# One power for both token tiles of a query/key group, and its mean squares first in line, in a four-layer trunk

## The chip, the core and the metric

The kernel runs on one core of a Trainium2 chip. TensorE (PE) does matrix products and transposes, VectorE (DVE), ScalarE (ACT) and GpSimd (POOL) the rest, SyncE (SP) issues the weight loads. Each engine works through its own queue in order and waits on semaphores for the others. The metric is the device time of one execution, in microseconds (us); smaller is better.

## The reference

Four pre-norm residual layers over an input of 256 tokens by 1024 features, in float32. Layers 0 and 3 are a gated MLP with a causal mix inside chunks of 128 tokens, layer 2 is causal pooling, and layer 1 is the attention layer that the change touches:

```python
def mixer_b(h, w_in, q_gain, k_gain, w_out):
    proj = h @ w_in
    qkv = proj[..., :n_qkv].reshape(bsz, S, 3, N_B_GROUPS, B_HEADS, HEAD_DIM)
    z = proj[..., n_qkv:]
    for g, (window, dilation) in enumerate(B_PATTERNS):        # 3 groups
        q = apply_partial_rotary(rms_norm(qkv[:, :, 0, g], q_gain[g]), cos, sin)
        k = apply_partial_rotary(rms_norm(qkv[:, :, 1, g], k_gain[g]), cos, sin)
        o, lse = dilated_window_attention(q, k, qkv[:, :, 2, g], window // dilation, dilation)
        ...
    # groups combined by softmax over lse, times silu(z), then @ w_out
```

`rms_norm` divides each head's 128 values of a token by the root of their mean square plus 1e-6 and multiplies by a gain. There are 8 heads and 3 groups, so 24 query heads and 24 key heads are normalised for each of the 256 tokens.

## The kernel before

**Products.** Every matrix product is made of three matmuls of fp32r halves (`mm3`, lines 77 to 79): each operand is split into a high part (written by ACT with a copy, `hi_of`, line 82) and a low part (what is left, written by DVE, `lo_of`, line 85). The weights come as 272 units of 512 KB: loaded by SP into four raw buffers (`wr`), split into `w<n>h` and `w<n>l` in seven buffers, and used by PE in order. The splitting runs five units ahead of the use (`AHEAD`).

**Order.** One Python program writes the instructions of all engines. PE's main stream is a row of projections; `step` is called after every six matmuls of 512 columns (or twelve of 256) and calls `tick`. Everything else is a task, a generator that hands out its next piece when its due tick has come: `tick` goes through the list of tasks in the order in which they were spawned, so an older task's piece stands ahead of a younger one's on each engine. After `tick`, `step` splits the next weight unit.

**The attention layer.** Heads go in four pairs (`hp` 0 to 3). For each pair PE projects queries and keys of the two heads for group 0, 1 and 2 (one `qk` projection each, both token tiles t=0 and t=1 of 128 tokens at once), then the values. Each `qk` projection spawns a `qk_task(hp, g, o)`, twelve in all; tiles are named by pair and group, so `qk10` is pair 1, group 0. A `qk_task` goes as follows, with the ticks between its pieces:

- `square(0)`, `square(1)`: ACT squares 128 columns of each of four heads and sums them (line 508; four `ACTIVATE` with four accumulator reads for each tile), into `qs`.
- two ticks later `rms(0)`, `rms(1)`: DVE makes mean squares `qm` from `qs` (line 512), POOL raises them to the power -0.5 into `qr` (line 513, a `tensor_tensor` with a constant tile). Each of both is done once for each token tile, on 128x4 values.
- one tick later `scale(0)`, then `scale(1)` with `rotate(0)`, then `rotate(1)`: ACT multiplies the four heads by `qr` into `qn` (line 517), DVE applies the rotary part (lines 526 to 531).
- two ticks later `transpose(0)`: PE transposes `qn` (line 538) into a PSUM tile `qt`, ACT writes the high part `qk..h` with the gain (line 540); a tick later `low(0)`: DVE writes the low part (line 546); a tick later `transpose(1)`, a tick later `low(1)`.

The PSUM tile `qt` comes from a tag with one buffer (`trp`). So PE's `transpose(1)` has to wait until DVE's `low(0)` of the same task has read the tile, and both stand two ticks apart.

Because one `qk` projection has eight ticks and a `qk_task` needs more than that, `low(1)` of one task and `rms` of the next fall due in the same tick, wherever two `qk` projections or a `qk` projection and a value projection follow each other. In the list the older task, with its `low(1)`, comes first.

Of the kernel before, what the change touches and what calls it, by code (L numbers as in the profile page):

```python
# [14 lines left out]
ALU = mybir.AluOpType  # L15
# [8 lines left out]
EPS = 1e-6  # L24
HD = 128
# [23 lines left out]
def hybrid_trunk_kernel(ctx, tc, x, wts, norm_gainT, a_v_gain, a_wsT, a_bsT, b_gl, b_gv, c_scaleT,  # L49
                        masks, rope, rcnt, out):  # L50
    nc = tc.nc
# [10 lines left out]
    def trp(name):  # L62
        return ps.tile([P, HALF], F32, tag="tr", name=name, bufs=1)
# [4 lines left out]
    def tiny(n, name, tag="t"):  # L68
        return cp.tile([P, n], F32, tag=f"{tag}{n}", name=name, bufs=8)

    def pair(pool, shape, tag, name, bufs):
        return (pool.tile(shape, F32R, tag=tag + "h", name=name + "h", bufs=bufs),
                pool.tile(shape, F32R, tag=tag + "l", name=name + "l", bufs=bufs))
# [15 lines left out]

    tasks = []  # L90
    now = [0]

    def spawn(gen, delay=0):
        if delay == 0:
            try:
                delay = next(gen)
            except StopIteration:
                return
        tasks.append([now[0] + delay, gen])

    def tick():
        now[0] += 1
        for e in list(tasks):
            if e[0] <= now[0]:
                try:
                    e[0] = now[0] + next(e[1])
                except StopIteration:
                    tasks.remove(e)
# [3 lines left out]
    def need(key):  # L112

        n = 0
        while key not in done:
            tick()
            n += 1
            assert n < 1000, (key, sorted(map(str, done)), [(e[1].__name__, e[1].gi_frame.f_lineno) for e in tasks])
# [44 lines left out]
    def step(i, ahead=AHEAD):  # L163

        tick()
        if i % 2 == 0:
            split_hi(used[0] + ahead)
        else:
            split_units(used[0] + ahead)
# [14 lines left out]
    m05_row = cp.tile([P, 32], F32, tag="m05", name="m05")  # L184
    nc.gpsimd.memset(m05_row, -0.5)
    m05 = m05_row[:, :4]
# [72 lines left out]
    def proj_tok(name, skew=None):  # L259

        o = [pp(f"{name}_{t}") for t in range(2)]
        if skew is not None:
            ws = [next_unit() for j in range(4)]
            for t in range(2):
                need(("h", skew, t))
                for k in range(KT):
                    w = ws[k // 2]
                    mm3(o[t], h_t(k, t), (w[0][:, k % 2], w[1][:, k % 2]), k == 0, k == KT - 1)
                    if k % 2:
                        tick()  # L270
                        if t == 1:
                            split_units(used[0] + min(k // 2 + 1, W_BUFS - 4))
            return o
        for j in range(4):
            w = next_unit()
            for kk in range(2):
                k = 2 * j + kk
                for t in range(2):
                    mm3(o[t], h_t(k, t), (w[0][:, kk], w[1][:, kk]), k == 0, k == KT - 1)
                step(kk)  # L280
        return o
# [74 lines left out]
    def layer_a(layer, consts, pl, mid):  # L356
# [3 lines left out]
        def tmp(tag, name, bufs):  # L360
            return pl.tile([P, HALF], F32, tag=tag, name=name, bufs=bufs)

        vs = [tiny(4, f"vs{layer}{t}") for t in range(2)]
        v = []
        wsr = []

# [123 lines left out]
    def layer_b(layer, consts, pl):  # L490
# [7 lines left out]
        def qk_task(hp, g, o):  # L498
            qh, ql = pair(pl, [P, 4, S], "qk", f"qk{hp}{g}", 4)
            qk[hp, g] = (qh, ql)  # L500
            ssq = [tiny(4, f"qs{hp}{g}{t}") for t in range(2)]
            rq = [tiny(4, f"qr{hp}{g}{t}") for t in range(2)]
            qn = [pl.tile([P, 4, HD], F32, tag="qn", name=f"qn{hp}{g}{t}", bufs=2) for t in range(2)]
            ov = [o[t].rearrange("p (h d) -> p h d", d=HD) for t in range(2)]

            def square(t):
                for h in range(4):
                    nc.scalar.activation(junk[:, :HD], ov[t][:, h], AF.Square, accum_out=ssq[t][:, h:h + 1])  # L508

            def rms(t):  # L510
                ms = tiny(4, f"qm{hp}{g}{t}")
                nc.vector.tensor_scalar(ms, ssq[t], 1.0 / HD, EPS, op0=ALU.mult, op1=ALU.add)  # L512
                nc.gpsimd.tensor_tensor(rq[t], ms, m05, op=ALU.pow)  # L513

            def scale(t):
                for h in range(4):
                    nc.scalar.activation(qn[t][:, h], ov[t][:, h], AF.Copy, scale=rq[t][:, h:h + 1])  # L517

            def rotate(t):

                ra = pl.tile([P, 4, ROPE], F32, tag="ra", name=f"ra{hp}{g}{t}", bufs=1)
                rb = pl.tile([P, 4, ROPE], F32, tag="rb", name=f"rb{hp}{g}{t}", bufs=1)
                for a in range(2):
                    hs = slice(2 * a, 2 * a + 2)
                    c = rop[:, 0, t, g, a:a + 1, :].to_broadcast([P, 2, ROPE])
                    nc.vector.tensor_tensor(ra[:, hs], qn[t][:, hs, :ROPE], c, op=ALU.mult)  # L526
                    for b in range(2):
                        s0, s1 = b * 16, (1 - b) * 16
                        c = rop[:, 1, t, g, a:a + 1, s0:s0 + 16].to_broadcast([P, 2, 16])
                        nc.vector.tensor_tensor(rb[:, hs, s0:s0 + 16], qn[t][:, hs, s1:s1 + 16], c, op=ALU.mult)  # L530
                nc.vector.tensor_tensor(qn[t][:, :, :ROPE], ra, rb, op=ALU.add)

            pts = [None, None]

            def transpose(t):
                pts[t] = trp(f"qt{hp}{g}{t}").rearrange("p (h c) -> p h c", c=P)
                for h in range(4):
                    nc.tensor.transpose(pts[t][:, h], qn[t][:, h], ident)  # L538
                for a in range(2):
                    nc.scalar.activation(qh[:, 2 * a:2 * a + 2, t * P:(t + 1) * P], pts[t][:, 2 * a:2 * a + 2],  # L540
                                         AF.Copy, scale=gv[:, 2 * g + a:2 * g + a + 1])

            def low(t):
                for a in range(2):
                    d = (slice(None), slice(2 * a, 2 * a + 2), slice(t * P, (t + 1) * P))
                    nc.vector.scalar_tensor_tensor(ql[d], pts[t][:, 2 * a:2 * a + 2], gv[:, 2 * g + a:2 * g + a + 1],  # L546
                                                   qh[d].bitcast(F32), op0=ALU.mult, op1=ALU.subtract)

            square(0)
            square(1)  # L550
            yield 2
            rms(0)
            rms(1)
            yield 1
            scale(0)
            yield 1
            scale(1)
            rotate(0)
            yield 1
            rotate(1)  # L560
            yield 2
            transpose(0)
            yield 1
            low(0)
            yield 1
            transpose(1)
            yield 1
            low(1)
            if g == NG - 1:
                spawn(score_task(hp, 0), 1)  # L570
                spawn(score_task(hp, 1), 3)
# [135 lines left out]
        for hp in range(NHEAD // 2):  # L707
            for g in range(NG):
                spawn(qk_task(hp, g, proj_tok(f"qk{hp}{g}", skew=layer if hp == 0 and g == 0 else None)))
                if hp == 0 and g == 0:  # L710
                    gate(0)
                    gate(1)
            o = proj_tok(f"v01{hp}")
            vh, vl = pair(pl, [P, 2, HALF], "v01", f"v01{hp}", 1)
            spawn(val_task(hp, o, vh, vl))
            vp = pp(f"v2p{hp}")
            for j in range(2):
                w = [a.rearrange("p a b -> p (a b)") for a in next_unit()]
                for kk in range(4):
                    k = 4 * j + kk  # L720
                    ws = [a[:, kk * 256:(kk + 1) * 256] for a in w]
                    for t in range(2):
                        mm3(vp[:, t * 256:(t + 1) * 256], h_t(k, t), ws, k == 0 and t == 0, k == KT - 1)
                    if kk % 2:
                        step(kk // 2)
            v2h, v2l = pair(pl, [P, 2, 256], "v2", f"v2{hp}", 1)
            spawn(val2_task(hp, vp, v2h, v2l))
            spawn(mix_task(hp, (vh, vl, v2h, v2l), szT[:, hp]), LAST_LAG if hp == NHEAD // 2 - 1 else MIX_LAG)
# [181 lines left out]
    with tc.tile_pool(name="L0", bufs=1, reuse_waits="tile") as pl:  # L910
        layer_a(0, consts, pl, after_ws)
# [5 lines left out]
    with tc.tile_pool(name="L3", bufs=1, reuse_waits="tile") as pl:  # L917
        layer_a(3, consts, pl, lambda: None)
# [137 lines left out]
```

## Time and profile before

| what | value |
| --- | --- |
| time, median of 3 runs | 845.04 us (844.78 to 845.1) |
| the profiled execution: its time | 844.66 us |
| its span, first to last instruction | 842.9 us |
| granted TensorE clock | 0.999 |
| PE busy | 831.3 us, 99% |
| DVE, ACT, POOL busy | 546.5, 488.6, 57.6 us |
| the attention layer's twelve `qk_task`s | about 206 to 463 us of the span |

In the profile, a group of instructions is told by its line, engine, operation and tiles (`out<-in`), with busy time, the mean duration in nanoseconds, and the idle time of the engine just before them with what ended it. In a timeline a row has start, duration (both us), engine, line, operation, tiles, and in brackets the idle time before it with what released it. A count `x2` joins neighbouring instructions of one kind into one row; such a row lasts from the first's start to the last's end. A matmul's duration reaches beyond the start of the next one, since they are pipelined, so what counts on PE is the distance from start to start.

### The profile page before, as it was taken

The page shows a single profiled execution, that of the slowest core. Times are in us where ns is not written, and L with a number is a line of the kernel's source. Part 1 is how long each engine was busy: PE and PEld are TensorE (multiplying, and loading weights), DVE is VectorE, ACT ScalarE, POOL GpSimd, SP SyncE. Part 2 cuts the span into 40 slices and gives each one's busy share as a digit, 9 for nine tenths or more (in the row PEclk, how much of TensorE's full clock was granted, in tenths as well). Part 3 has the DMA queues.
Part 4 walks back from the last instruction along what each step waited for, and adds up shares of the span by engine and source line. Part 5 has one row for each costly group of instructions (what it writes and reads, how often), then busy time and mean ns, then how long its engine had stood idle before and what let it go on. Part 6 is the DMA issues. An engine that isn't in the chain of part 4 may idle for free.

```text
span 842.9 us, 12424 instructions
## 1 busy us (share of the span) xinstructions
PE 831.3 (99%) x4600; PEld 718.2 (85%) x4600; DVE 546.5 (65%) x932; ACT 488.6 (58%) x918; POOL 57.6 (7%) x79
## 2 busy tenths in 40 slices
PE   8999999999999999999999999999999999999998
PEld 6888888888988888888888889999988888888886
DVE  6876556646747667667668576798754776556551
ACT  7665444336758677677678567446543666434340
POOL 1301000001001021021021012000000000000000
PEclk9999999999999999999999999999999999999999
DMA  8766564552754346345345267546664466454541
GB/s 303 271 203 224 190 198 164 187 193 84 254 174 163 112 147 179 121 151 175 126 150 173 78 220 252 181 150 229 218 204 149 138 245 208 158 183 167 175 149 51
DMA packets 41500, 149.57 MB, mean 177 GB/s; under 512 B 4864, under 2 KB 4880, under 8 KB 41184
## 3 DMA queue, kind: packets, MB, share of 16 engines
q1 hardware_dynamic: 40320, 144.72, 51.8%
q0 software_dynamic: 976, 4.05, 1.4%
q8 instruction: 36, 0.59, 0.3%
q14 instruction: 24, 0.20, 0.1%
q10 hardware_dynamic: 144, 0.02, 0.0%
HBM read 147.72 MB, written 1.05 MB: 176 GB/s over the span
## 4 chain that ended last, share of the span: by engine, by line
PE 86%; ACT 7%; DVE 2%; issue 2%; POOL 2%; DMA 0%; POOLq 0%; DVEq 0%; ACTq 0%
PE wo L77 6%; PE wo L79 6%; PE wo L78 6%; PE qk L79 4%; PE qk L77 4%; PE qk L78 4%; PE z L79 3%; PE z L77 3%; PE u L77 3%; PE z L78 3%; PE u L78 3%; PE u L79 3%; PE v L78 3%; PE v L79 3%; PE v L77 3%; ACT junk L508 2%
## 5 line engine op out<-in xcount | busy, mean ns | idle before, releaser
L513 POOL TENSOR_TENSOR qr<-qm,m 128x4 f32<-128x4 f32 x24 | 30.3, 1272 | 224.2 <-DVE qm L512 224.2
L517 ACT ACTIVATE qn<-qk,qr 128x128 f32<-128x128 f32 x96 | 27.5, 382 | 15.1 <-POOL qr L513 15.1
L508 ACT ACTIVATE junk<-qk 128x128 bf16<-128x128 f32 x96 | 26.8, 279 | 7.3 <-PE qk L79 4.6
L430 DVE TENSOR_TENSOR sz<-u,sz 128x512 f32<-128x512 f32 x16 | 11.0, 685 | 28.2 <-PE u L79 28.2
L232 ACT ACTIVATE hT<-hp,gT 128x128 fp32r<-128x128 f32 x64 | 17.5, 383 | 16.1 <-PE hp L227 16.1
L212 POOL TENSOR_TENSOR r<-ms,m 128x1 f32<-128x1 f32 x8 | 5.4, 670 | 284.8 <-DVE ms L210 284.8
L327 DVE TENSOR_TENSOR x<-wo,x 128x512 f32<-128x512 f32 x16 | 11.0, 690 | 20.1 <-PE wo L79 20.0
L235 DVE SCALAR_TENSOR_TENSOR hT<-hp,gT,hT 128x128 fp32r<-128x128 f32 x64 | 17.9, 343 | 7.7 <-ACT hT L232 7.7
L372 ACT ACTIVATE junk<-v 128x512 bf16<-128x512 f32 x16 | 9.6, 600 | 17.8 <-PE v L79 17.6
L508 ACT ACTIVATION_READ_ACCUMULATOR junk<-qk 128x1 f32 x96 | 19.1, 199 | 0.0
L373 DVE TENSOR_TENSOR vv<-v,kc 128x512 f32<-128x512 f32 x16 | 10.8, 688 | 12.4 <-ACT junk L372 12.2
L526 DVE TENSOR_TENSOR ra<-qn,kcb 128x64 f32<-128x64 f32 x48 | 10.6, 221 | 12.0 <-ACT qn L517 10.9
L456 ACT ACTIVATE sz<-z 128x512 f32<-128x512 f32 x16 | 9.5, 598 | 15.3 <-PE z L79 14.7
L538 PE MATMUL qt<-ident,qn 128*128 128x128 f32 x96 | 14.6, 274 | 3.4 <-DVE qk12l L546 0.5
L538 PEld LDWEIGHTS qt<-ident,qn 128*128 128x128 f32 x96 | 11.3, 140 | 7.3 <-issue 2.7
L205 ACT ACTIVATE junk<-x 128x512 bf16<-128x512 f32 x16 | 10.2, 639 | 11.0 <-DVE x L327 9.4
L433 DVE SCALAR_TENSOR_TENSOR yy<-mx,bs,sz 128x256 f32<-128x256 f32 x32 | 14.0, 480 | 0.6
L608 ACT ACTIVATE p<-p,rl 128x384 f32<-128x384 f32 (+1 forms) x16 | 11.5, 769 | 4.8 <-DVE rl L607 4.8
L530 DVE TENSOR_TENSOR rb<-qn,kcb 128x32 f32<-128x32 f32 x96 | 13.7, 183 | 0.0
L604 ACT ACTIVATE p<-p,nb 128x768 f32<-128x768 f32 x8 | 7.5, 938 | 7.9 <-DVE nb L603 7.9
L512 DVE TENSOR_SCALAR qm<-qs 128x4 f32<-128x4 f32 x24 | 3.3, 164 | 12.8 <-ACT junk L508 12.8
L352 POOL TENSOR_SCALAR_AFFINE_SELECT kc<-kc 128x128 f32<-128x128 f32 x16 | 10.0, 659 | 14.1 <-DMA kc<-in_a_wsT_dram 14.1
(2770 smaller groups left out, 3257.8 us busy)
## 6 DMA issues: line engine op xcount, KB each, us to landing
wr<-in_wts_dram SPq DMA_DIRECT2D x272, 512.0 KB, 4.1
kc<-in_a_v_gain_dram POOLq DMA_DIRECT2D x2, 1024.0 KB, 6.4
x<-in_x_dram SPq DMA_DIRECT2D x4, 256.0 KB, 4.7
kc<-in_a_wsT_dram POOLq DMA_DIRECT2D x2, 512.0 KB, 8.2
out_dram<-x SPq DMA_DIRECT2D x4, 256.0 KB, 2.0
kcb<-in_masks_dram POOLq DMA_DIRECT2D x1, 576.0 KB, 8.0
kcb<-in_b_gl_dram POOLq DMA_DIRECT2D x1, 192.0 KB, 5.9
kcb<-in_rope_dram POOLq DMA_DIRECT2D x1, 64.0 KB, 7.9
```

Of the source, the lines that this page charges most:

```text
L77: nc.tensor.matmul(out_ap, lh[0], rh[0], start=start, stop=False, skip_group_check=True)
L78: nc.tensor.matmul(out_ap, lh[0], rh[1], start=False, stop=False, skip_group_check=True)
L79: nc.tensor.matmul(out_ap, lh[1], rh[0], start=False, stop=stop, skip_group_check=True)
L232: nc.scalar.activation(hTh[:, k, sl], pts[k // 4][:, k % 4], AF.Copy, scale=gT[:, layer, k:k + 1])
L235: nc.vector.scalar_tensor_tensor(hTl[:, k, sl], pts[k // 4][:, k % 4], gT[:, layer, k:k + 1], hTh[:, k, sl].bitcast(F32), op0=ALU.mult, op ...
L433: nc.vector.scalar_tensor_tensor(y[:, sl], mxs[n][t][:, sl], bsT[:, 2 * n + gg:2 * n + gg + 1], us[t][:, sl], op0=ALU.add, op1=ALU.mult)
L508: nc.scalar.activation(junk[:, :HD], ov[t][:, h], AF.Square, accum_out=ssq[t][:, h:h + 1])
L513: nc.gpsimd.tensor_tensor(rq[t], ms, m05, op=ALU.pow)
L517: nc.scalar.activation(qn[t][:, h], ov[t][:, h], AF.Copy, scale=rq[t][:, h:h + 1])
L530: nc.vector.tensor_tensor(rb[:, hs, s0:s0 + 16], qn[t][:, hs, s1:s1 + 16], c, op=ALU.mult)
L538: nc.tensor.transpose(pts[t][:, h], qn[t][:, h], ident)
L608: nc.scalar.activation(f, f, AF.Copy, scale=rl[i][:, 0:1])
```

## The change

`rms` is no longer a piece that the task hands out itself. The task leaves it in a slot, `rms_due`, with its due tick, and `tick` runs what is in the slot before it goes through the list of tasks. `qs`, `qm` and `qr` become one tile of eight columns for both token tiles (one tile each in place of two), so that `rms` is one DVE instruction and one POOL instruction on 128x8. The tile `vs` of the other layers takes the first four columns of an eight-column tile.

```diff
@@ tick @@
         now[0] += 1
+        if rms_due[0] and rms_due[0][0] <= now[0]:
+            rms_due[0][1]()
+            rms_due[0] = None
         for e in list(tasks):
@@ layer_a @@
-        vs = [tiny(4, f"vs{layer}{t}") for t in range(2)]
+        vs = [tiny(8, f"vs{layer}{t}")[:, :4] for t in range(2)]
@@ qk_task @@
-            ssq = [tiny(4, f"qs{hp}{g}{t}") for t in range(2)]
-            rq = [tiny(4, f"qr{hp}{g}{t}") for t in range(2)]
+            ssqs, rqs = (tiny(8, f"q{a}{hp}{g}") for a in "sr")
+            ssq, rq = ([a[:, 4 * t:4 * t + 4] for t in range(2)] for a in (ssqs, rqs))
...
-            def rms(t):
-                ms = tiny(4, f"qm{hp}{g}{t}")
-                nc.vector.tensor_scalar(ms, ssq[t], 1.0 / HD, EPS, op0=ALU.mult, op1=ALU.add)
-                nc.gpsimd.tensor_tensor(rq[t], ms, m05, op=ALU.pow)
+            def rms():
+                ms = tiny(8, f"qm{hp}{g}")
+                nc.vector.tensor_scalar(ms, ssqs, 1.0 / HD, EPS, op0=ALU.mult, op1=ALU.add)
+                nc.gpsimd.tensor_tensor(rqs, ms, m05_row[:, :8], op=ALU.pow)
...
             square(0)
             square(1)
-            yield 2
-            rms(0)
-            rms(1)
-            yield 1
+            rms_due[0] = (now[0] + 2, rms)
+            yield 3
+            assert rms_due[0] is None
             scale(0)
```

What this does to the queues: PE's and ACT's order of instructions is the same as before. On POOL twelve powers of 128x8 stand where 24 of 128x4 stood. On DVE one `qm` stands where two stood, and at seven of the twelve places it also moves. One of the seven is the task `qk11` (pair 1, group 1), while `qk10` is finishing. DVE's queue there before (`wr` is a raw weight buffer, `w103l` a weight unit's low part; the number behind a name is a buffer's):

```order
L85 TENSOR_TENSOR w102l<-wr_2783,w102h 128x1024
L546 SCALAR_TENSOR_TENSOR qk10l<-qt_2957,gv,qk10h 128x2x128 x2
L512 TENSOR_SCALAR qm_2975<-qs_2935 128x4
L512 TENSOR_SCALAR qm_2978<-qs_2936 128x4
L85 TENSOR_TENSOR w103l<-wr_2839,w103h 128x1024
```

And now (the lines are three or four further down in the changed source, so line 550 is what was 546, and 516 what was 512):

```order
L85 TENSOR_TENSOR w102l<-wr_2768,w102h 128x1024
L516 TENSOR_SCALAR qm_2951<-qs_2915 128x8
L550 SCALAR_TENSOR_TENSOR qk10l<-qt_2935,gv,qk10h 128x2x128 x2
L85 TENSOR_TENSOR w103l<-wr_2819,w103h 128x1024
L530 TENSOR_TENSOR ra_2982<-qn_2917,kcb 128x64
```

The mean squares have moved ahead of the two instructions of `low(1)` of `qk10`; the same is so in `qk02`, `qk12`, `qk21`, `qk22`, `qk31` and `qk32`. At the other five places (group 0 of every pair, and `qk01`) no older `low(1)` is due in that tick, and the two only become one. DVE's queue around `qk01` before:

```order
L85 TENSOR_TENSOR w84l<-wr_2125,w84h 128x1024
L512 TENSOR_SCALAR qm_2236<-qs_2205 128x4
L512 TENSOR_SCALAR qm_2239<-qs_2206 128x4
L85 TENSOR_TENSOR w85l<-wr_2147,w85h 128x1024
L526 TENSOR_TENSOR ra_2268<-qn_2209,kcb 128x64
```

And now:

```order
L85 TENSOR_TENSOR w84l<-wr_2120,w84h 128x1024
L516 TENSOR_SCALAR qm_2229<-qs_2200 128x8
L85 TENSOR_TENSOR w85l<-wr_2142,w85h 128x1024
L530 TENSOR_TENSOR ra_2258<-qn_2202,kcb 128x64
L534 TENSOR_TENSOR rb_2259<-qn_2202,kcb 128x2x16 x2
```

Here nothing has changed places; the first power now needs the squares of both token tiles, where before it needed those of tile 0 alone.

More of the change, by code (lines that the diff above doesn't have):

```diff
@@ L91, in hybrid_trunk_kernel @@
     now = [0]
+    rms_due = [None]
     def spawn(gen, delay=0):
```

## The prediction

> **What bounds the kernel now.** I read the page's shares and costliest groups first, then who waits for the transposes of the queries and keys, then the timeline around one such wait.
>
> ```profile
> span 842.9 us, 12424 instructions
> ...
> PE 831.3 (99%) x4600; PEld 718.2 (85%) x4600; DVE 546.5 (65%) x932; ACT 488.6 (58%) x918; POOL 57.6 (7%) x79
> ...
> L517 ACT ACTIVATE qn<-qk,qr 128x128 f32<-128x128 f32 x96 | 27.5, 382 | 15.1 <-POOL qr L513 15.1
> ```
>
> PE bounds the kernel with 99% of the span, so a change that leaves PE's work alone can only win what PE stands still. POOL is idle most of the time, and still ACT waits for its powers, 15.1 us in all. Whether that reaches PE is told by those who wait for the `qt` tiles:
>
> ```profile
>   PE qt L538: 3.4, 7
> ```
>
> Seven times PE waits at a transpose, 3.4 us in sum. Here is one of the seven, in pair 1, group 1, from the squares to the wait (timeline of all engines):
>
> ```profile
> 308.48 0.19 ACT L508 ACTIVATION_READ_ACCUMULATOR junk<-qk 128x1 f32 x1
> ...
> 309.28 1.07 ACT L82 ACTIVATE w103h<-wr 128x1024 fp32r<-128x1024 f32 x1
> ...
> 309.44 0.87 DVE L546 SCALAR_TENSOR_TENSOR qk10l<-qt,gv,qk10h 128x256 fp32r<-128x256 f32 x2 [2.56 <-ACT qk10h L540]
> ...
> 310.23 0.23 DVE L512 TENSOR_SCALAR qm<-qs 128x4 f32<-128x4 f32 x2
> ...
> 310.38 1.23 DVE L85 TENSOR_TENSOR w103l<-wr,w103h 128x1024 fp32r<-128x1024 f32 x1
> ...
> 310.56 2.90 POOL L513 TENSOR_TENSOR qr<-qm,m 128x4 f32<-128x4 f32 x2 [13.02 <-DVE qm L512]
> ...
> 312.51 1.14 ACT L517 ACTIVATE qn<-qk,qr 128x128 f32<-128x128 f32 x4 [2.15 <-POOL qr L513]
> ...
> 315.07 0.60 PE L538 MATMUL qt<-ident,qn 128*128 128x128 f32 x4
> ...
> 315.47 1.11 ACT L82 ACTIVATE w105h<-wr 128x1024 fp32r<-128x1024 f32 x1
> ...
> 316.42 0.89 ACT L540 ACTIVATE qk11h<-qt,gv 128x256 fp32r<-128x256 f32 x2
> ...
> 316.77 1.22 DVE L85 TENSOR_TENSOR w105l<-wr,w105h 128x1024 fp32r<-128x1024 f32 x1
> ...
> 317.91 0.87 DVE L546 SCALAR_TENSOR_TENSOR qk11l<-qt,gv,qk11h 128x256 fp32r<-128x256 f32 x2
> 318.04 0.40 PE L79 MATMUL v<-w102h,hT 128*128 128x512 f32 x1
> ...
> 318.92 0.63 PE L538 MATMUL qt<-ident,qn 128*128 128x128 f32 x4 [0.48 <-DVE qk11l L546]
> ...
> 319.31 0.48 PE L77 MATMUL v<-w102h,hT 128*128 128x512 f32 x1
> ```
>
> The squares end at 308.67. The mean squares wait in DVE's queue behind `low(1)` of `qk10`, which itself waits 2.56 us for ACT, and start at 310.23. ACT has nothing it may do from 310.35 to 312.51. From there ACT works without a gap to `qk11h`, DVE comes out with `low(0)` of `qk11` at 318.78, and only then may PE reuse the one `qt` buffer: 0.14 us later, at 318.92. So the late power reaches PE.
>
> **What one wait costs PE.** The same two transposes of `qk10`, twelve matmuls of 512 columns apart like those above, do not wait:
>
> ```profile
> 303.20 0.60 PE L538 MATMUL qt<-ident,qn 128*128 128x128 f32 x4
> ...
> 303.83 0.84 ACT L540 ACTIVATE qk10h<-qt,gv 128x256 fp32r<-128x256 f32 x2 [0.78 <-PE qt L538]
> ...
> 304.70 0.88 DVE L546 SCALAR_TENSOR_TENSOR qk10l<-qt,gv,qk10h 128x256 fp32r<-128x256 f32 x2 [0.23 <-ACT qk10h L540]
> ...
> 306.15 0.39 PE L79 MATMUL qk<-w98h,hT 128*128 128x512 f32 x1
> ...
> 306.38 0.60 PE L538 MATMUL qt<-ident,qn 128*128 128x128 f32 x4
> ...
> 306.73 0.48 PE L77 MATMUL qk<-w98h,hT 128*128 128x512 f32 x1
> ```
>
> Start to start, `qk10` goes 306.15, 306.38, 306.73: 0.58 from the matmul ahead to the one behind. `qk11` goes 318.04, 318.92, 319.31: 1.27. The wait costs 0.69, more than the 0.48 that the row calls idle, since a modelled end covers the rest. With seven waits of 3.4 us together, 0.49 each, this is 7 x 0.69 = 4.8 us. If the modelled end hid nothing of what it covers, 3.4 us would be the sum; I take 4.8, since starts are measured and ends are not, and keep 3.4 as the low bound of the gain.
>
> **The change part by part.**
>
> *Moving `qm` at seven places.* In the new order `qm` needs the squares alone. Their end is 308.67 and DVE is idle then (the 2.56 us), so nothing is pushed back; `low(1)` of `qk10` starts at 309.44 as before. How fast the rest follows, and what a power costs, stands in `qk01`, where nothing is ahead of `qm`, and in the groups of POOL's lines:
>
> ```profile
> 244.68 0.19 ACT L508 ACTIVATION_READ_ACCUMULATOR junk<-qk 128x1 f32 x1
> ...
> 244.91 0.17 DVE L512 TENSOR_SCALAR qm<-qs 128x4 f32<-128x4 f32 x1 [1.43 <-ACT junk L508]
> ...
> 245.22 1.01 POOL L513 TENSOR_TENSOR qr<-qm,m 128x4 f32<-128x4 f32 x1 [0.59 <-DVE qm L512]
> ...
> 245.72 0.61 ACT L517 ACTIVATE qn<-qk,qr 128x128 f32<-128x128 f32 x2
> ...
> 245.86 1.23 DVE L85 TENSOR_TENSOR w85l<-wr,w85h 128x1024 fp32r<-128x1024 f32 x1 [0.78 <-ACT w85h L82]
> ```
>
> ```profile
> L513 POOL TENSOR_TENSOR qr<-qm,m x24: 1000/1007/1919, 208.3 to 453.0; 128x4 f32<-128x4 f32 x24
> ```
>
> ```profile
> L212 POOL TENSOR_TENSOR r<-ms,m x8: 547/556/1473, 5.8 to 656.2; 128x1 f32<-128x1 f32 x8
> ```
>
> From the end of the squares (244.87) to the power's start (245.22) are 0.35 us, so in `qk11` the power starts at 308.67 + 0.35 = 309.02 in place of 310.56.
>
> *One power of 128x8 for two of 128x4.* The trace has no 128x8 power. Bounds: 1.01 us if four more columns are free, 2.02 if they cost as much as a second power. I take the slope between one and four columns, (1007 - 556)/3 = 150 ns a column: 1007 + 4 x 150 = 1.61 us. The end is then 310.63 (310.03 to 311.04), where the first power ended at 312.46 before. Part of that was no work: the 1.9 us power started 0.18 us after DVE's `w103l`, against 1.01 us in `qk01`, where no such subtraction was under way when it began. Now it begins 1.36 us ahead of `w103l`, which waits for `w103h` until 310.35 in any case. A subtraction that starts inside a power changes neither: `w85l` came 0.64 us into the one at 245.22, which took 1.01, and `w85l` 1.23.
>
> The Trainium skill, SBUF — State Buffer, § Who interferes with whom, says that a DVE instruction with two SBUF inputs and a GpSimd one that reads SBUF exclude each other, and that the first holds the ports for its whole length. The 1.92 against 1.01 us agrees with the first half; the 1.23 us of `w85l` under a power does not show the second. By the second half, `w103l` would be held 0.25 us until 310.63 and end at 311.86, which DVE's queue has room for ahead of 315, so the sum would stay; and a power that began first could not be caught, so that the slower rival below could not be.
>
> *What ACT and PE make of it.* ACT starts `scale(0)` at 310.67 in place of 312.51, 1.84 us earlier (1.47 at a power of 2.02; at 1.01 `w103h` at 310.35 sets it). Everything that ACT does up to `w105h` follows, which so is done at 316.42 - 1.84 = 314.58 (by the start of the next one). PE's `transpose(0)` at 315.07 stays, PE sets it. From here `qk11` goes as `qk10` does: high part 0.63 us behind the transpose's start (315.70), low part 0.87 behind that (316.57) and 0.88 long: 317.45. PE is due at 318.04 + 0.23 = 318.27, less the 0.14: there is 0.68 us to spare. What is late next is thus PE itself. To clear the wait, the chain must gain 0.65 us, which holds for any power that ends by 311.81, a length of 2.8 us.
>
> *The five places where `qm` doesn't move.* The power ends later, since it waits for both tiles and is longer:
>
> ```profile
> 210.60 1.01 POOL L513 TENSOR_TENSOR qr<-qm,m 128x4 f32<-128x4 f32 x1 [1.30 <-DVE qm L512]
> ...
> 296.53 1.01 POOL L513 TENSOR_TENSOR qr<-qm,m 128x4 f32<-128x4 f32 x1 [0.59 <-DVE qm L512]
> ```
>
> ```profile
> 213.06 1.13 ACT L517 ACTIVATE qn<-qk,qr 128x128 f32<-128x128 f32 x4
> ```
>
> ```profile
> 299.01 1.12 ACT L517 ACTIVATE qn<-qk,qr 128x128 f32<-128x128 f32 x4
> ```
>
> In `qk00` it ends at 212.21 and in `qk10` at 298.14 (`qk20` and `qk30` alike), ahead of the `scale(0)` at 213.06 and 299.01, which other things hold: nothing. In `qk01` ACT started `scale(0)` at 245.72; now 246.83, 1.1 us later (1.5 at 2.02). What covers this:
>
> ```profile
> 252.45 0.84 ACT L540 ACTIVATE qk01h<-qt,gv 128x256 fp32r<-128x256 f32 x2 [2.67 <-PE qt L538]
> ```
>
> ACT stands idle 2.67 us there ahead of `qk01h`, waiting for PE. Without that cover the transposes of `qk01` would be up to 1.1 us late, once.
>
> *Fewer instructions.* Twelve `qm` (0.17 us) and twelve powers go, on engines with idle time at those places: nothing. No DMA and nothing on SP's queue moves.
>
> **Sum.** 844.66 (842.9 of span and 1.76 around it) - 7 x 0.69 = 839.8 for the profiled execution. It lies 0.38 under the median of 845.04; carried over to the median I forecast 840.2, a gain of 0.57%. With 3.4 it is 841.6.
>
> **Rivals.**
>
> *Part is given back at the scores.* With PE 0.69 us earlier at `transpose(1)`, the scores that follow group 2 come earlier by as much:
>
> ```profile
> 269.65 0.86 DVE L546 SCALAR_TENSOR_TENSOR qk02l<-qt,gv,qk02h 128x256 fp32r<-128x256 f32 x2
> ...
> 270.84 0.22 PE L77 MATMUL s<-qk00h 128*128 128x128 f32 x1
> ```
>
> `low(1)` ends at 270.51, 0.33 ahead. If it didn't move, PE would wait 0.69 - 0.33 + 0.14 = 0.50 in each of four pairs, and the time would be 842.2. Against it: `low(1)` follows `transpose(1)`, which moves with PE, and ACT's and DVE's work ahead of it follows the earlier power. I give 0.13 to this or to any like partial gain, at 842.2.
>
> *Slower: the second half of the power is caught.* If the power read its later columns in a second go, 1.36 us or more behind its start, it would be held there until `w103l` ends at 311.61. The 1.9 us power ended 0.86 behind that point; with 0.60 for four more columns it would end at 313.07, 0.61 later than before, and seven longer waits of PE make 845.04 + 4.3 = 849.3. For it: such a hold is seen, 1.92 us. Against it: `w85l`, 0.64 us into a power, did it nothing, and by the slope all eight columns are read within 1.2 us. It decides from a power that ends after 312.47, 3.45 us long. I give 0.05.
>
> *No change.* A wait that only moves: if ACT's chain were held elsewhere, by raw weights that land later than 311.7 or by PE, the early power would buy nothing: 845.0. Against it: ACT's chain behind 312.51 has no gap that any row names. I give 0.08.
>
> **How the numbers follow.** A measurement here tells about 0.2%, 1.7 us, from no change. Full gain 0.74 at 840.2, partial 0.13 at 842.2, no change 0.08, slower 0.05: faster 0.87, same 0.08, slower 0.05. The likeliest case runs from 839.4 (0.3 for the spread of the runs and 0.5 for what else a smooth PE may save) to 841.6 (the low bound of the gain); with the partial one the range is 839.4 to 842.6.
>
> **What would show it.** Right: no wait of PE at the transposes of `qk02` to `qk32`, twelve powers of 1.4 to 2.0 us, ACT waiting some 0.3 us for each at the seven places and about 1.1 in `qk01`, `low(0)` ending 0.5 us or more ahead of `transpose(1)`. Wrong: powers over 2.8 us, or a new wait of PE at the scores or the probabilities' transposes.

## The result, and the profile after

The changed kernel takes 840.1 us (median of 4 runs, 840.07 to 840.45) against 845.07 (4 runs, 844.78 to 845.11): 5.0 us less, a ratio of 0.9941 with a 95% interval of 0.9925 to 0.9957. The forecast was 840.2. Of all executions told of here one stands apart, at 2975 us in the run with a power of 24 columns, whose median is 853.46 us without it and 853.62 with it.

The lines of the page that answer to those of before:

```profile
span 838.7 us, 12381 instructions
...
PE 830.3 (99%) x4600; PEld 718.9 (86%) x4600; DVE 547.0 (65%) x920; ACT 489.4 (58%) x918; POOL 42.1 (5%) x67
...
PE 97%; DMA 1%; DVE 1%; ACT 0%; issue 0%; SPq 0%; POOL 0%
...
L517 POOL TENSOR_TENSOR qr<-qm,m 128x8 f32<-128x8 f32 x12 | 19.7, 1638 | 227.9 <-DVE qm L516 227.9
...
L521 ACT ACTIVATE qn<-qk,qr 128x128 f32<-128x128 f32 x96 | 27.6, 382 | 3.4 <-POOL qr L517 3.4
...
L542 PE MATMUL qt<-ident,qn 128*128 128x128 f32 x96 | 14.4, 272 | 0.0
```

Twelve powers last 1.64 us each, ACT waits 3.4 us for them in place of 15.1, and PE's idle time ahead of the `qt` transposes is 0.0. The third line is the chain that ended last. In the page of before it read:

```profile
PE 86%; ACT 7%; DVE 2%; issue 2%; POOL 2%; DMA 0%; POOLq 0%; DVEq 0%; ACTq 0%
```

ACT, DVE and POOL have all but left the chain: it is PE's. (The shares of such a chain are not what can be won: 14% of the span before ran over other steps than PE's, and the change won 0.6%.) The timeline around `qk11` (all engines), to be held against the one in the prediction:

```profile
308.67 0.20 ACT L512 ACTIVATION_READ_ACCUMULATOR junk<-qk 128x1 f32 x1
...
308.96 0.17 DVE L516 TENSOR_SCALAR qm<-qs 128x8 f32<-128x8 f32 x1 [1.90 <-ACT junk L512]
309.21 1.64 POOL L517 TENSOR_TENSOR qr<-qm,m 128x8 f32<-128x8 f32 x1 [10.93 <-DVE qm L516]
...
309.63 0.88 DVE L550 SCALAR_TENSOR_TENSOR qk10l<-qt,gv,qk10h 128x256 fp32r<-128x256 f32 x2 [0.49 <-ACT qk10h L544]
310.57 1.22 DVE L85 TENSOR_TENSOR w103l<-wr,w103h 128x1024 fp32r<-128x1024 f32 x1
310.89 1.15 ACT L521 ACTIVATE qn<-qk,qr 128x128 f32<-128x128 f32 x4 [0.34 <-POOL qr L517]
...
313.85 1.11 ACT L82 ACTIVATE w105h<-wr 128x1024 fp32r<-128x1024 f32 x1
...
315.26 0.60 PE L542 MATMUL qt<-ident,qn 128*128 128x128 f32 x4
...
315.89 0.84 ACT L544 ACTIVATE qk11h<-qt,gv 128x256 fp32r<-128x256 f32 x2 [0.93 <-PE qt L542]
...
316.77 0.88 DVE L550 SCALAR_TENSOR_TENSOR qk11l<-qt,gv,qk11h 128x256 fp32r<-128x256 f32 x2 [0.39 <-ACT qk11h L544]
...
318.22 0.39 PE L79 MATMUL v<-w102h,hT 128*128 128x512 f32 x1
...
318.46 0.60 PE L542 MATMUL qt<-ident,qn 128*128 128x128 f32 x4
...
318.81 0.48 PE L77 MATMUL v<-w102h,hT 128*128 128x512 f32 x1
```

The mean squares start 0.1 us behind the squares, in a gap of DVE. The power is done before `w103l` has got far, ACT waits 0.34 us for it, and now the bracket at `qk11h` says that ACT waits for PE, 0.93 us: the order of who waits for whom has turned round. `low(0)` ends at 317.65, 0.81 ahead of `transpose(1)`, which comes 0.24 behind the matmul ahead of it, without a wait.

Where the time came from is told by PE's first and last of these transposes. Before:

```profile
218.04 0.60 PE L538 MATMUL qt<-ident,qn 128*128 128x128 f32 x4
...
459.49 0.63 PE L538 MATMUL qt<-ident,qn 128*128 128x128 f32 x4 [0.51 <-DVE qk32l L546]
```

After:

```profile
218.85 0.60 PE L542 MATMUL qt<-ident,qn 128*128 128x128 f32 x4
...
455.49 0.60 PE L542 MATMUL qt<-ident,qn 128*128 128x128 f32 x4
```

From the first to the last are 241.45 us before and 236.64 after: 4.81 us less, seven times 0.687. The profiled execution of after stood 0.81 us behind already at the first of them, from a longer wait in the first layer's start, which the change doesn't touch (ACT waited 2.29 us for the first weight unit's DMA ahead of `w0h`, against 1.14); its span (4.2 us less) therefore shows less than the medians (5.0).

### The profile page after: what moved, and what is told of

Read it like the earlier page. It is cut to its first block, busy times and chain, and to the rows that moved or that the text cites. A ratio compares the mean times of both kernels' runs of the same rounds, so it can differ in the third digit from the quotient of the medians.

```text
span 838.7 us, 12381 instructions
## 1 busy us (share of the span) xinstructions
PE 830.3 (99%) x4600; PEld 718.9 (86%) x4600; DVE 547.0 (65%) x920; ACT 489.4 (58%) x918; POOL 42.1 (5%) x67
## 4 chain that ended last, share of the span: by engine, by line
PE 97%; DMA 1%; DVE 1%; ACT 0%; issue 0%; SPq 0%; POOL 0%
PE wo L77 6%; PE wo L79 6%; PE wo L78 6%; PE qk L79 5%; PE qk L77 5%; PE qk L78 5%; PE v L79 5%; PE v L78 5%; PE v L77 5%; PE z L79 3%; PE z L77 3%; PE z L78 3%; PE u L77 3%; PE u L78 3%; PE u L79 3%; PE cz L78 2%
## 5 line engine op out<-in xcount | busy, mean ns | idle before, releaser
L517 POOL TENSOR_TENSOR qr<-qm,m 128x8 f32<-128x8 f32 x12 | 19.7, 1638 | 227.9 <-DVE qm L516 227.9
L516 DVE TENSOR_SCALAR qm<-qs 128x8 f32<-128x8 f32 x12 | 2.1, 172 | 26.8 <-ACT junk L512 26.8
L642 PE MATMUL pt<-ident,p 128*128 128x128 f32 x48 | 9.9, 274 | 0.0
```

Of the source, the lines that this page charges most:

```text
L517: nc.gpsimd.tensor_tensor(rqs, ms, m05_row[:, :8], op=ALU.pow)
```

## The experiments

Two theories stood against each other at first: what counts is that the power *starts* earlier (the move), or that there is *one* power in place of two (the merging). Then, by what road the late power reaches PE, and how late it may be. The positions below are PE's start-to-start from the first `qt` transpose to the last, as above; by that number the start-up of an execution drops out.

**Moving alone.** Two mean squares and two powers of 128x4, run from the slot:

```diff
-            yield 2
-            rms(0)
-            rms(1)
-            yield 1
+            rms_due[0] = (now[0] + 2, lambda: (rms(0), rms(1)))
+            yield 3
             scale(0)
```

> The mean squares run from the slot ahead of the other tasks, but as two 128x4 instructions on DVE and two 128x4 powers on POOL (moving alone, no merging). My theory: only the earlier start counts. The first power ends at about 310.03 in qk11 (309.02 + 1.01), so ACT starts scale(0) when w103h is done, the seven waits go, and the time is 840.1 (839.8 to 840.5), 5.0 under before. Rival (the gain comes from one power in place of two): the waits stay and the time is near 845.

Measured: 840.31 us, 0.9937 of before (0.9925 to 0.995). From first to last transpose 236.64 us, the same as with the merged power to the last digit. The powers of `qk11` in POOL's timeline:

```profile
307.64 1.01 POOL L517 TENSOR_TENSOR qr<-qm,m 128x4 f32<-128x4 f32 x1 [9.96 <-DVE qm L516]
309.23 1.01 POOL L517 TENSOR_TENSOR qr<-qm,m 128x4 f32<-128x4 f32 x1 [0.59 <-DVE qm L516]
```

The first starts even earlier than expected, since it needs only tile 0's squares. So the move makes the whole gain, and the merging adds nothing that the times or the positions show.

**Merging alone.** One power of 128x8, in the task's own turn:

```diff
-            rms_due[0] = (now[0] + 2, rms)
-            yield 3
+            yield 2
+            rms()
+            yield 1
             scale(0)
```

> One 128x8 mean square and one 128x8 power, but in the task's own turn, behind the older task's low(1) (merging alone, no moving). My theory: the power starts 0.2 us behind DVE's weight subtraction at the seven places as before, is held until that ends (311.61 in qk11) and lasts 0.86 + 0.63 beyond it: end 313.10, scale(0) 0.6 us later than before, seven waits of 1.3 us in place of 0.69, time 849.5 (848 to 850.5). Rival (merging brings the gain, nothing holds a power): it ends 1.64 after 310.56, scale(0) 0.27 earlier, time 843.2.

Measured: 849.58 us, 1.005 of before (1.0037 to 1.0062): merging alone makes the kernel slower, by what the theory gave. The power's lengths (minimum, median, maximum in ns), and the place at `qk11`:

```profile
L517 POOL TENSOR_TENSOR qr<-qm,m x12: 1637/2568/2572, 210.9 to 455.3; 128x8 f32<-128x8 f32 x12
```

```profile
311.34 1.23 DVE L85 TENSOR_TENSOR w103l<-wr,w103h 128x1024 fp32r<-128x1024 f32 x1
311.49 2.57 POOL L517 TENSOR_TENSOR qr<-qm,m 128x8 f32<-128x8 f32 x1 [12.43 <-DVE qm L516]
...
314.09 1.14 ACT L521 ACTIVATE qn<-qk,qr 128x128 f32<-128x128 f32 x4 [2.79 <-POOL qr L517]
...
320.51 0.63 PE L542 MATMUL qt<-ident,qn 128*128 128x128 f32 x4 [0.95 <-DVE qk11l L550]
```

Seven powers last 2.57 us and five 1.64. The seven are those that start 0.15 us behind a weight subtraction, so the hold of 0.93 us is the same for eight columns as it was for four (1.92 against 1.01 before). ACT waits 2.79 us in place of 2.15, PE's idle is 0.95 in place of 0.48. The expectation had the sum at one place right, 1.3 us, but put all of it at `transpose(1)`: from the matmul ahead to the one behind, PE loses 1.14 us there at `qk11` (1.73 against 0.59 without a wait) and 0.16 already at `transpose(0)` (0.75 against 0.59), which starts 0.15 behind the end of the rotated `qn`.

**A second buffer for `qt`, powers left late.** The kernel before, with one line changed:

```diff
-                pts[t] = trp(f"qt{hp}{g}{t}").rearrange("p (h c) -> p h c", c=P)
+                pts[t] = (atp if t and g else trp)(f"qt{hp}{g}{t}").rearrange("p (h c) -> p h c", c=P)
```

> The kernel before, but transpose(1) of groups 1 and 2 writes a PSUM tile of the other tag (three buffers, used by scores and mixing), so that it needs not wait for low(0). The powers stay late. My theory: PE's seven waits go although ACT waits for POOL as before (15 us in all), which shows that the one buffer is what hands the late power on; low(0) and low(1) stay late. If the scores wait for the whole low part, PE waits some 0.4 us at the scores in each of four pairs and the time is 842.0; if only for the part of tile 0, 840.3. Rival (the late power costs PE time by other ways than this buffer): nothing gained, 845.

Measured: 840.91 us, 0.9948 of before (0.9934 to 0.9962). ACT still waits for the powers as long as before (group of `qn`):

```profile
L517 ACT ACTIVATE qn<-qk,qr 128x128 f32<-128x128 f32 x96 | 27.6, 382 | 15.1 <-POOL qr L513 15.1
```

And yet PE waits nowhere at `transpose(1)`. So the late power cost PE time by way of the one buffer, and nearly all of ACT's 15.1 us cost nothing by themselves. Two details of this run. PE doesn't wait at the scores:

```profile
269.91 0.86 DVE L546 SCALAR_TENSOR_TENSOR qk02l<-qt,gv,qk02h 128x256 fp32r<-128x256 f32 x2
270.45 0.22 PE L77 MATMUL s<-qk00h 128*128 128x128 f32 x1
...
271.17 0.28 PE L78 MATMUL s<-qk02l,qk02h 128*128 128x128 f32 x1
```

PE starts them at 270.45 while `low(1)` of `qk02` runs until 270.77. But the first scores are those of group 0, which read `qk00`; the first that reads `qk02l` starts at 271.17, 0.40 behind the end of `low(1)`. By the source it reads tile 0's columns alone; whether it would have to wait for the whole low part is not shown, since nothing came late here. And the gain is not whole: 237.55 us from first to last transpose, 0.91 more than in the changed kernel. This is lost in group 2 of pairs 1 to 3, at `transpose(0)`:

```profile
326.29 0.40 PE L79 MATMUL v<-w105h,hT 128*128 128x512 f32 x1
326.35 0.29 DVE L531 TENSOR_TENSOR qn<-ra,rb 128x128 f32<-128x128 f32 x1
...
326.79 0.63 PE L538 MATMUL qt<-ident,qn 128*128 128x128 f32 x4
```

The start is 0.50 behind the matmul ahead, against 0.23 without a wait, and 0.15 behind the end of the rotated `qn`. With the matmul behind it, which also comes a little later, this makes 0.30 us, 0.9 in three places. PE, no longer held at `transpose(1)`, comes early enough here to meet `qn` itself late: a second road from the late power to PE, which the wait at `transpose(1)` hid before.

**Moving in group 1 alone.**

```diff
-            yield 2
-            rms(0)
-            rms(1)
-            yield 1
+            if g == 1:
+                rms_due[0] = (now[0] + 2, lambda: (rms(0), rms(1)))
+                yield 3
+            else:
+                ...
             scale(0)
```

> As the first of these, but only for group 1 of each pair; groups 0 and 2 keep the old turn. My theory: each of the seven waits stands for itself, three of them go (qk11, qk21, qk31), the time is 845.07 - 3 x 0.69 = 843.0, and PE still waits 0.5 us at each of the four in group 2. Rival (group 2 inherits its wait from group 1, since ACT runs without a gap from one to the other): all seven shrink, 840 to 841.5.

Measured: 842.95 us, 0.9972 of before (0.9961 to 0.9983). PE's waits at the transposes, of all that are left:

```profile
PE qt L542 <- DVE qk02l L550: 0.5, 1, 0.5
PE qt L542 <- DVE qk22l L550: 0.5, 1, 0.5
PE qt L542 <- DVE qk12l L550: 0.5, 1, 0.5
PE qt L542 <- DVE qk32l L550: 0.5, 1, 0.5
```

From first to last transpose 239.28 us, 2.17 less than before, 0.72 for each of the three. So each wait stands all but for itself: group 2 of pairs 1 to 3 loses 0.64 us in place of 0.70, from the matmul ahead to the one behind, so it inherits some 0.06 from group 1. The rival's reason, that ACT runs without a gap from one to the other, isn't so. ACT stands idle for 2.16 us ahead of `qk12`'s `scale(0)`, in this run as in the kernel before, whose row is:

```profile
325.14 1.14 ACT L517 ACTIVATE qn<-qk,qr 128x128 f32<-128x128 f32 x4 [2.16 <-POOL qr L513]
```

**How late may the power be?** The changed kernel with a wider power, whose further results are not used. It measures the spare of the chain that the prediction put at 0.68 us behind `low(0)`, and whether a long power is caught by a subtraction that starts under it:

```diff
-            ssqs, rqs = (tiny(8, f"q{a}{hp}{g}") for a in "sr")
+            ssqs, rqs = tiny(8, f"qs{hp}{g}"), tiny(16, f"qr{hp}{g}")
...
-                nc.gpsimd.tensor_tensor(rqs, ms, m05_row[:, :8], op=ALU.pow)
+                nc.gpsimd.tensor_tensor(rqs.rearrange("p (a c) -> p a c", c=8),
+                                        ms.rearrange("p (a c) -> p a c", c=8).to_broadcast([P, 2, 8]),
+                                        m05_row[:, :16].rearrange("p (a c) -> p a c", c=8), op=ALU.pow)
```

> The changed kernel with a power twice as wide (128x16: the eight mean squares are read twice, the second eight results are not used). It measures how much later the power might end, and whether a long power is caught by the weight subtraction that starts 1.36 us behind its start. My theory: length 1.64 + 8 x 0.157 = 2.89 us at all twelve places, ACT's scale(0) 1.25 us later than in the changed kernel. The spare there is 1.16 us: low(0) is held by PE's transpose(0) and not by ACT for 0.49, and ended 0.67 before PE needs it. So PE waits about 0.1 us at seven places, time 840.7 (840.0 to 841.5). Rival (later columns are read in a second go and are held until the subtraction ends): 3.2 to 3.9 us long at the seven places against 2.89 at the other five, time 842.8 to 847.

Measured: 841.19 us, 0.9955 of before (0.9942 to 0.9967). All twelve powers are of one length:

```profile
L517 POOL TENSOR_TENSOR qr<-qm,m x12: 2900/2902/2915, 210.6 to 446.3; 128x16 f32<-128x16 f32 x12
```

```profile
317.45 0.40 PE L79 MATMUL v<-w102h,hT 128*128 128x512 f32 x1
...
317.80 0.63 PE L544 MATMUL qt<-ident,qn 128*128 128x128 f32 x4
```

PE starts 0.35 behind the matmul ahead in place of 0.23, too little for the profile to name a wait. From first to last transpose it is 237.68 us, 1.04 over the changed kernel, 0.15 for each of seven: 2.9 us is just beyond what fits. No power is caught.

The same with 24 columns:

> As the one with 16 columns, with 24. My theory: length 4.15 us, scale(0) 2.5 us later than in the changed kernel, 1.35 over the spare, so seven waits of 1.35 us, and about 0.65 at group 0 of pairs 1 to 3 and 0.5 to 1 once at qk01 too: 840.1 + 9.4 + 1.9 + 0.7 = 852 (849.5 to 853.5). Rival (the spare is larger than worked out, or another engine gives way): under 847. If the reads are caught: over 854.

Measured: 853.46 us, 1.0098 of before (1.0082 to 1.0113), at the upper end of the range that was given. The same kernel once more, for its trace:

> The same kernel with 24 columns once more, for its trace. From the measured 853.6 (13.5 over the changed kernel): theory, PE waits at the transposes at the seven places (1.2 to 1.4 us of lost start-to-start each), at group 0 of pairs 1 to 3 (0.6 to 0.8 each) and at qk01 (0.5 to 1.5); no wait of PE at the scores or mixes. Rival: PE waits in other places too, at the scores or for weights.

Measured: 852.99 us in one run. From its timeline:

```profile
308.61 0.63 PE L544 MATMUL qt<-ident,qn 128*128 128x128 f32 x4 [0.47 <-DVE qk10l L552]
...
311.35 4.16 POOL L517 TENSOR_TENSOR qr<-qm,m 128x24 f32<-128x24 f32 x1 [9.19 <-DVE qm L516]
...
312.71 1.23 DVE L85 TENSOR_TENSOR w103l<-wr,w103h 128x1024 fp32r<-128x1024 f32 x1
...
321.97 0.63 PE L544 MATMUL qt<-ident,qn 128*128 128x128 f32 x4 [0.95 <-DVE qk11l L552]
```

Now group 0 waits too (`qk10`, `qk20`, `qk30`, 0.5 us idle each) and `qk01` (0.6); the seven wait 0.9 to 1.0. Between the two transposes of `qk11` PE loses 1.14 us start to start against the changed kernel, less than the 1.2 to 1.4 expected; another 0.32 goes at its `transpose(0)`, by the second road, which the expectation didn't have. No wait of PE at scores or mixes is named.

No version beats the changed kernel: the move alone is equal to it, and in both the profile names no wait of PE for another engine after the first 17 us.

## Why the prediction was right

*The price of one wait.* Forecast 0.69 us from start-to-start distances, measured 4.81/7 = 0.687 (0.64 to 0.70 at the single places, from the matmul ahead to the one behind). The row's own 0.48 would have given 3.4 us for the seven. The choice between the two was the largest one in the sum, and the distance between starts was right, in the main for the reason given. At `qk11` the modelled end of the last matmul covers 0.17 of the missing 0.21 (its row is 0.40 long, the next start without a wait 0.23 behind its own); the other 0.04 is that the matmul behind a transpose that waited comes 0.39 after it in place of 0.35.

*The mechanism.* An earlier power was to clear PE's wait. It did so at all seven places, and the runs bear it out step by step: the move alone gives all, the merging alone gives none and costs 4.2 us, a second buffer gives most with the powers still late, and a power too late by other means brings the waits back.

*The power's length.* Forecast 1.61, measured 1.64, between the bounds of 1.01 and 2.02. With 2.90 at 16 columns and 4.16 at 24 the cost is 157 to 158 ns a column from four columns on, a little over the 150 that the slope from one to four gave.

*The spare.* Forecast 0.68 us behind `low(0)`; 317.65 against 318.46, less 0.14 from `low(0)`'s end to PE's start, is 0.67. The limit of 2.8 us for the power's length, worked out from before, is borne out: 1.64 costs nothing, 2.90 costs 0.15 us a place.

*The five other places.* Forecast about 1.1 us more of waiting for ACT at `qk01`, hidden by its wait for PE. It waited 1.01 us there, and its wait ahead of `qk01h` fell from 2.67 to 1.53. The 3.4 us on the group's line are this and seven times 0.34.

*The profiled execution.* Forecast 839.8, measured 840.45. The 0.81 us of slower start, which no term of the sum has, is more than the difference; some 0.2 came back behind the last of the transposes. With a start-up that moves by so much, that the medians agree to 0.1 us (840.2 and 840.1) is in part luck; what the sum had right is the 4.8.

*The rivals.* The partial gain by way of the scores was priced from the wrong row: the score at 270.84 is one of group 0 and doesn't read `qk02l`. The first that does, in the trace of before:

```profile
271.57 0.27 PE L78 MATMUL s<-qk02l,qk02h 128*128 128x128 f32 x1
```

This is 1.06 behind the end of `low(1)` at 270.51 and not 0.33. With PE 0.69 earlier and `low(1)` unmoved it would still have come in time, so by these rows it had nothing to cost. There was another partial way that the prediction didn't see, `transpose(0)` meeting a late `qn`. It showed where the power stayed late and PE was freed (the second buffer), and where the power came later still (merging alone, 24 columns). The slower rival has its hold right and its place wrong. A power is held when it starts under a running subtraction, also at eight columns. A subtraction that starts under a running power doesn't hold it, even where 2.8 of the power's 4.16 us are still to come. *No change* fell with ACT's chain, which did move: `w105h` starts at 313.85 in place of 315.47.

## What to carry to other kernels

Where an engine's idle time grows in front of a cheap instruction on an otherwise idle engine, ask what stands ahead of its input in the queue of the engine that makes it, and move the input: here a 0.17 us instruction, moved into a gap, was worth 5 us, while making the slow instruction wider without moving it cost 4. A wait counts only where it reaches the bounding engine, here by a PSUM tile with one buffer; all but 0.9 us of what ACT's 15 us of waiting cost PE went when that tile had a second one. Price a wait of TensorE by the distance between starts, and look at the spare behind the next releaser before counting on the whole of it.

## What the runs showed of the hardware

A power on POOL that starts 0.15 to 0.18 us behind a DVE subtraction with two SBUF inputs is held by 0.9 us, at all seven places where this happens (1.92 against 1.01 us for 128x4, 2.57 against 1.64 for 128x8). All these starts lie at nearly the same point of the subtraction, so whether the hold lasts until its end or for a fixed time isn't shown. The reverse was not seen: `w103l`, which starts 1.36 us into the power, took 1.22 us in the changed kernel, where the power has 0.28 us left, and 1.23 with the power of 4.16 us, as `w104l` does with POOL idle, and the power kept its length. The Trainium skill, SBUF — State Buffer, § Who interferes with whom, has both instructions exclude each other for the whole length of the first. The first half agrees with the hold; the second doesn't agree with these rows, unless the power's reading is over long before its end, which no run here tells apart.
